# Moving the products of the first stage and the sums of the last two quads in a Strassen matmul with logsumexp

## The chip, the cores and the metric

The kernel runs on one core of a Trainium2 chip. The metric is the device time of one execution in microseconds (us). Three runs of the kernel before gave 423.86, 423.88 and 424.39 us.

## The reference

```python
m, k, n = 1024, 4096, 4096
def reference(a: np.ndarray, b: np.ndarray) -> np.ndarray:
    x = np.matmul(a, b)
    return special.logsumexp(x, axis=-1).astype(np.float32)
```

A is 1024 x 4096 and B is 4096 x 4096, both float32 with normal entries. The output is one number for each of the 1024 rows.

## The kernel before

**Tiles.** A has eight row tiles of 128 rows (m = 0 to 7), B has eight column blocks of 512 (nb = 0 to 7), and the inner dimension has 32 slices of 128 (k). Loads convert to float16. The sum over k stands in PSUM as float32; from each finished 128 x 512 piece VectorE takes the maximum (`lse_max`, L89, kept negative in `negmax`) and ScalarE the sum of exponentials (`lse_exp`, L94). At the end the pieces of a row are put together (`combine`).

**Head, block 0 (L255 to L326).** A must be transposed for TensorE. Its first six row tiles arrive in pieces of 128 rows x 4 slices. `arrivals` lists for each group of four slices (a round, eight rounds in all): A tile 0, B slices 0 and 1, A tile 1, B slices 2 and 3, A tiles 2 to 5. So there are 64 arrivals, eight a round. A piece of A is transposed by four TensorE instructions (`transpose_group`, L209) into one of two PSUM tiles in turn; even ones are copied out by VectorE (L220), odd ones by ScalarE (L222). `behind` then issues the products that an arrival makes possible (`plain`, L227: 128 x 128 by 128 x 512, one for each slice and row tile), and VectorE's sums of quarters of A (`a_sums_early`, `a_sums_late`), which the later blocks need. How far `behind` stays after the transposes is the lag: the list `back`. `warm` issues products of zeros while there is nothing else. The loads go out on POOL's queue, at most 12 pieces of A ahead, since they use 12 staging slots in `tb`.

**Strassen blocks (L334 to L578).** From block 1 on, two row tiles, a pair of slices and the two halves of a block of B are taken as 2 x 2 matrices. Seven products instead of eight suffice, each from sums of quarters. A quad q is two row tiles by one block: four quarters c11, c12 (one PSUM tile, `r0`) and c21, c22 (another, `r1`), each 128 x 256. Its products m1, m5, m2, m6, m3, m4, m7 have 16 instructions each (L395), about 1.745 us for one and 12.2 us for a quad. The quarters of A with their sums stay in `aT`, `s1`, `s2` and `s5`. The sums of B are made by VectorE, block by block, with `make`: t1 for m1, t6 for m6, t4 for m4 into `T1`, `T6`, `T4` (parts of `tb`), t3 for m3 and t7 for m7 in place in the loaded block. Each comes in four parts of 128 x 1024. t3 must follow t6, and t7 must follow t4 and t1, as they overwrite their inputs.

**Work around one quad.** ScalarE copies `r0` to `e` (L466) and c21 to `s` (L470), then `flush` issues the exponentials of the quad before (L94), then come the copies of c12 (L544) and c21 (L546) after m3 and m4. VectorE adds and subtracts in `s` (L480, L481), then `sub(x, x, s)`, the adds into c22 and c11 and the two maxima. `s` has one buffer for all quads. All of this is in an order written out by hand (`manual_schedule`); each engine takes its instructions in this order.

**Steps.** Step 0 is block 1 with quads 0 to 2, the first four products of the three quads interleaved as B arrives ("joint"). Steps 1 to 6 are blocks 2 to 7 with quads 0 to 3. Quad 3 consists of row tiles 6 and 7, which come later by a DMA transpose. Steps 7 and 8 are quad 3 of blocks 0 and 1, which are loaded again: block 0 (`again0`) with its sums in the space of `s1`, `s2` and `s5`, block 1 (`again1`, called `last`) with its data in the space of `aT` and its sums in `tb`. `early` is step 6, `joined` step 7, `tail` the last quad of a step whose following block's sums are made in it, `final` step 8.

**The order around the change.** In the last quad of step 0, VectorE makes the rest of block 2's sums; t7 and the maxima wait in `deferred` until the first add and subtract of the next quad. For the last two quads the sums are spread: in step 6 t1, t6 and t3 of block 0 follow quad 1, t4 comes in quad 2 and t7 behind it; three quarters of t1 and t6 of block 1 come in quad 3, with the last quarters; t3, t4 and t7 of block 1 come in step 7.

Of the kernel before, what the change touches and what calls it, by code (L numbers as in the profile page):

```python
# [13 lines left out]
def kernel(  # L14
# [19 lines left out]
    MT, KT, NB = M // P, K // P, N // FD  # L34
    MP, KP = MT // 2, KT // 2
    G = 4
    GI = KP // G
# [44 lines left out]
    def add(o, x, y):  # L82
        nc.vector.tensor_tensor(out=o, in0=x, in1=y, op=ALU.add)  # L83

    def sub(o, x, y):
        nc.vector.tensor_tensor(out=o, in0=x, in1=y, op=ALU.subtract)  # L86

    def lse_max(pt, m, nb):
        nc.vector.tensor_reduce(  # L89
            out=negmax[:, m, nb : nb + 1], in_=pt, axis=AX.X, op=ALU.max, negate=True  # L90
        )

    def lse_exp(pt, m, nb, scale=1.0):
        nc.scalar.activation(  # L94
            out=pt,
            in_=pt,
            func=AF.Exp,
            bias=negmax[:, m, nb : nb + 1],
            scale=scale,
            accum_out=tsum[:, m, nb : nb + 1],  # L100
        )
# [29 lines left out]
    class Block:  # L131
# [10 lines left out]
        def load(self, lo, hi):  # L142
            nc.gpsimd.dma_start(  # L143
                out=self.raw[lo // GI][:, lo % GI : lo % GI + hi - lo],
                in_=b_rows[:, lo:hi, :, ts(self.nb, FD)],
            )
# [56 lines left out]
    def transpose_group(k0, kn, m):  # L203
        src = stg.pop((k0, m))
        n = count[0]
        count[0] += 1
        pst = tps[n % 2]
        for j in range(kn):
            nc.tensor.matmul(  # L209
                pst[:, ts(j, P)],  # L210
                src[:, ts(j, P)],
                ident,
                is_transpose=True,
                start=(j == 0),
                stop=(j == kn - 1),
            )
        dst = aT[:, k0 // 2 : (k0 + kn) // 2, :, m // 2, m % 2, :]
        v = pst[:, 0 : kn * P].rearrange("p (i t c) -> p i t c", t=2, c=P)
        if n % 2 == 0:
            nc.vector.tensor_copy(out=dst, in_=v)  # L220
        else:
            nc.scalar.copy(out=dst, in_=v)  # L222
# [3 lines left out]
    def plain(pt, i, kp, m):  # L226
        nc.tensor.matmul(  # L227
            pt,
            aT[:, i, kp, m // 2, m % 2, :],
            blk0.raw[i // GI][:, i % GI, kp, :],  # L230
            start=(done[m] == 0),
            stop=(done[m] == KT - 1),
        )
        done[m] += 1

    def a_sums_early(r, q):
        a11, a12 = aT[:, r, 0, q, 0, :], aT[:, r, 1, q, 0, :]
        a21, a22 = aT[:, r, 0, q, 1, :], aT[:, r, 1, q, 1, :]
        add(s1[:, r, q], a11, a22)
        add(s2[:, r, q], a21, a22)  # L240
        add(s5[:, r, q], a11, a12)

    def a_sums_late(r, q):
        a11, a12 = aT[:, r, 0, q, 0, :], aT[:, r, 1, q, 0, :]
        a21, a22 = aT[:, r, 0, q, 1, :], aT[:, r, 1, q, 1, :]
        sub(a21, a21, a11)
        sub(a12, a12, a22)

    def first_max(m):
        lse_max(acc[m // 2][m % 2], m, 0)  # L250
        lse_exp(acc[m // 2][m % 2], m, 0)
# [13 lines left out]
    def behind(k0, kn, what, x):  # L265

        if what == "a":
            have_a.setdefault(k0, []).append(x)
            todo = [(k, x) for k in range(k0, k0 + kn) if k in have_b]
        else:  # L270
            have_b.update({k0: 1, k0 + 1: 1})
            todo = [(k, m) for k in (k0, k0 + 1) for m in have_a.get(x, [])]
        for k, m in todo:
            plain(acc[m // 2][m % 2], k // 2, k % 2, m)
        r = slice(k0 // 2, (k0 + kn) // 2)
        if what == "a":
            if x >= 3 and in_place:
                a_sums_late(*in_place.pop(0))
            if x % 2 == 1 and k0 + kn < KT:
                a_sums_early(r, x // 2)  # L280
            if x == 5:
                in_place.extend([(r, 0), (r, 1), (r, 2)])
            if k0 + kn == KT and x == 4:
                first_max(0)
                first_max(1)
                for what in ("t1", "t6"):
                    blk1.make(what, 0, 2)

    def warm(n):
        for _ in range(n):  # L290
            nc.tensor.matmul(acc[2][1], zeros[:, 0:P], zeros[:, 0:FD], start=True, stop=True)  # L291
# [17 lines left out]
    back = []  # L309
    for n, (k0, kn, what, x) in enumerate(arrivals):  # L310
        while coming and (coming[0][2] == "b" or loads[0] < count[0] + NSLOT):
            load(*coming.pop(0))
            if not coming:
                for lo in range(0, KP, 2):
                    blk1.load(lo, lo + 2)
        if what == "a":
            transpose_group(k0, kn, x)
        if k0 < KN and x < 3:
            warm(1)
        if len(back) == min(3, 1 + n // 8):  # L320
            behind(*back.pop(0))
        back.append((k0, kn, what, x))
    while back:
        behind(*back.pop(0))
    for m in range(2, MT - 2):
# [2 lines left out]


    pending = []  # L330
    deferred = []

    def flush():
        for f in pending:  # L334
# [9 lines left out]
    plan = [(lambda: blk1, range(MP - 1))]  # L344
# [3 lines left out]
    blk, nxt = None, blk1  # L348
    for step, (_, qs) in enumerate(plan):
        blk, nxt = nxt, None  # L350
        nb = blk.nb
        more = step + 1 < len(plan)
        early = more and plan[step + 1][0] is again0
        if more:
            if plan[step + 1][0] is again1:
                nxt = last
            else:
                nxt = plan[step + 1][0]()
# [24 lines left out]
        for q in qs:  # L383
# [5 lines left out]
            r0, r1 = quads[q]  # L389
# [11 lines left out]
                        skip_group_check=True,  # L401
                    )

            joined = step == len(plan) - 2
            tail = more and not early and not joined and q == qs[-1]
            final = not more
            if final:
                c22 = psum_pool.tile([P, FD], f32, name="c22", tag="ps")[:, 0:H]  # L410

# [59 lines left out]
            flush()  # L471
            if tail and not joint:
                nxt.make("t1")
            if early and q == MP - 1:
                for g in range(G - 1):
                    last.make("t1", g * GI, (g + 1) * GI)
            if joined:
                for what in ("t3", "t4"):
                    last.make(what)
            add(s[:, 2], s[:, 2], e[:, 1])  # L480
            sub(s[:, 0], s[:, 2], e[:, 0])  # L481
            for f in deferred:
                f()
            deferred.clear()
            if early and q == MP - 2:
                nxt.make("t4")
            if early and q == MP - 1:
                for g in range(G - 1):
                    last.make("t6", g * GI, (g + 1) * GI)
                for what in ("t1", "t6"):  # L490
                    last.make(what, KP - GI, KP)
            if joined:
                last.make("t7")
            if joint and q + 1 in quads:
                e_next = fix_pool.tile([P, 2, H], f32, name=f"e_{q}", tag="e")
                nc.scalar.copy(out=e_next, in_=halves(quads[q + 1][0]))
# [35 lines left out]
                sub(lg[:, m0:MT], lg[:, m0:MT], nmmin[:, m0:MT])  # L532
                continue
            if joint:
                for what in ("t1", "t6", "t3") if q == 0 else ("t1", "t6"):
                    nxt.make(what, q * GI, (q + 1) * GI)
            elif tail:
                nxt.make("t6")
                nxt.make("t3")
            if step == 1 and q == 2:  # L540
                a_sums_early(slice(KP // 2, KP), MP - 1)
                a_sums_late(slice(KP // 2, KP), MP - 1)
# [4 lines left out]
            m7(c11)  # L547
            sub(x, x, s[:, 0::2])
            add(c22, c22, x[:, 0])

            def maxima(r1=r1, r0=r0, q=q, nb=nb):
                for r, m in ((r1, 2 * q + 1), (r0, 2 * q)):
                    lse_max(r, m, nb)
                    pending.append(lambda r=r, m=m: lse_exp(r, m, nb))

            add(c11, c11, x[:, 1])
            if joint and tail:
                for what in ("t1", "t6"):
                    nxt.make(what, 3 * GI, KP)
                for g in range(1, G):  # L560
                    nxt.make("t3", g * GI, (g + 1) * GI)
                nxt.make("t4")
                deferred.extend([lambda b=nxt: b.make("t7"), maxima])
            else:
                if tail:
                    nxt.make("t4")
                    nxt.make("t7")
                maxima()
            if early and q == 1:
                for what in ("t1", "t6", "t3"):  # L570
                    nxt.make(what)
            if early and q == MP - 2:
                nxt.make("t7")
            if step == 1 and q == 1:
                a_sums_early(slice(0, KP // 2), MP - 1)
                a_sums_late(slice(0, KP // 2), MP - 1)
            if early and q == 1:
                last = again1().load_all()  # L578
# [32 lines left out]
```

## Time and profile before

| | |
|---|---|
| median of three runs | 423.88 us |
| the profiled execution | 424.39 us, span 422.6 us |
| TensorE products, weight loads | 412.7 us (98%), 348.4 us (82%) |
| VectorE, ScalarE, POOL | 258.7 us, 109.3 us, 74.3 us |
| first Strassen product starts | 62.83 us |
| step 1 starts | 99.57 us |
| step 7, step 8 start | 393.09 us, 405.31 us |
| last TensorE product ends | 417.7 us |

The span runs from the first to the last instruction. PE is TensorE, DVE is VectorE, ACT is ScalarE, PEld is TensorE's weight load. A line of the timeline has start and length in us, the engine, the line of the kernel, the operation, what it writes and reads, and in brackets how long the engine was idle ahead of it and what ended that. A line of the waits has the waiting engine, tile and line, what it waited for, the total in us, how often and the longest. A line of the chain of waits has start, length and the step.

### The profile page before, as it was taken

How to read it: one execution, taken by the hardware profiler on the slowest of the kernel's cores; microseconds unless marked ns; L12 is line 12 of the kernel's file. 1: busy time of each engine (PE TensorE's matmuls, PEld its weight loads, DVE VectorE, ACT ScalarE, POOL GpSimd, SP SyncE). 2: the span in 40 equal slices, each digit the busy share in tenths (PEclk: the TensorE clock that was granted, in tenths of full speed). 3: DMA queues.
4: the chain of work that ended last, by engine and by line, in shares of the span. 5: the costliest groups of instructions: out<-in, count | busy, mean ns of one | idle time of the engine just before them, and what ended most of it. 6: DMA issues, size and time to landing. Idle time of an engine off the chain costs nothing.

```text
span 422.6 us, 8529 instructions
## 1 busy us (share of the span) xinstructions
PE 412.7 (98%) x3647; PEld 348.4 (82%) x3647; DVE 258.7 (61%) x571; ACT 109.3 (26%) x278; POOL 74.3 (18%) x117
## 2 busy tenths in 40 slices
PE   6989999999999999999999999999999999999995
PEld 2545558888888888888888888888888888888884
DVE  1466777979646793257812694336832587299954
ACT  1222242132132221122222212222221222222223
POOL 7667763101001030003000030001100030110000
PEclk9999999999999999999999999999999999999999
DMA  8999999999999499102990079400990039799000
GB/s 117 197 201 199 202 205 207 207 207 215 190 195 187 69 169 207 24 2 41 207 152 2 2 115 208 79 2 2 192 205 3 2 62 207 132 199 198 3 2 0
DMA packets 57845, 52.97 MB, mean 125 GB/s; under 512 B 10192, under 2 KB 57296, under 8 KB 57808
## 3 DMA queue, kind: packets, MB, share of 16 engines
q0 software_dynamic: 49344, 50.34, 72.4%
q1 hardware_dynamic: 8464, 2.10, 3.5%
q8 instruction: 28, 0.46, 0.4%
q14 instruction: 9, 0.07, 0.1%
HBM read 100.66 MB, written 2.10 MB: 243 GB/s over the span
## 4 chain that ended last, share of the span: by engine, by line
PE 92%; DMA 4%; POOL 1%; DVE 1%; ACT 1%; issue 0%; DVEq 0%; ACTq 0%; POOLq 0%
DMA tb<-in_a_dram 3%; PE acc_1_0_1342 L395 2%; PE acc_1_0_764 L395 2%; PE acc_3_0_4470 L395 2%; PE acc_0_0_3386 L395 2%; PE acc_1_0_2974 L395 2%; PE acc_3_0_2150 L395 2%; PE acc_0_0_1766 L395 2%; PE acc_0_0_762 L395 2%; PE acc_1_0_4054 L395 2%; PE acc_2_0_3642 L395 2%; PE acc_3_0_4334 L395 2%; PE acc_0_0_3926 L395 2%; PE acc_3_0_2690 L395 2%; PE acc_2_0_2562 L395 2%; PE acc_0_0_1210 L395 2%
## 5 line engine op out<-in xcount | busy, mean ns | idle before, releaser
L395 PEld LDWEIGHTS <-aT 128*128 128x128 f16 x1856 | 181.5, 98 | 21.2
L395 PEld LDWEIGHTS <-s_71 128*128 128x128 f16 x464 | 45.4, 98 | 5.5
L395 PEld LDWEIGHTS <-s_73 128*128 128x128 f16 x464 | 45.4, 98 | 5.3
L395 PEld LDWEIGHTS <-s_72 128*128 128x128 f16 x464 | 45.4, 98 | 5.3
L209 PEld LDWEIGHTS <-tb 128*128 128x128 f16 x192 | 14.1, 98 | 16.5 <-DMA tb<-in_a_dram 8.2
L198 POOL DMA_DIRECT2D tb<-in_a_dram x48 | 26.0, 545 | 6.0 <-issue 2.1
L227 PEld LDWEIGHTS <-aT 128*128 128x128 f16 x192 | 16.8, 98 | 11.9 <-ACT aT L222 0.3
L220 DVE COPY aT<-tps_97 128x512 f16<-128x512 f16 x24 | 10.2, 425 | 25.4 <-PE tps_97 L209 25.2
L222 ACT COPY aT<-tps_98 128x512 f16<-128x512 f16 x24 | 14.0, 585 | 44.1 <-PE tps_98 L209 44.1
L86 DVE TENSOR_TENSOR aT<-aT 128x256 f16<-128x256 f16 (+1 forms) x56 | 16.2, 344 | 0.0
L209 PE MATMUL tps_97<-ident,tb 128*128 128x128 f16 x96 | 9.3, 220 | 2.8 <-DMA tb<-in_a_dram 2.8
L209 PE MATMUL tps_98<-ident,tb 128*128 128x128 f16 x96 | 9.3, 219 | 1.0 <-DMA tb<-in_a_dram 1.0
L83 DVE TENSOR_TENSOR s_71<-aT 128x256 f16<-128x256 f16 (+1 forms) x26 | 8.2, 317 | 3.0 <-ACT aT L222 2.0
L143 POOL DMA_DIRECT2D b_0_2838<-in_b_dram x1 | 0.9, 890 | 45.4 <-PE acc_3_0_2690 L395 45.4
L143 POOL DMA_DIRECT2D b_0_2298<-in_b_dram x1 | 0.9, 878 | 45.4 <-PE acc_3_0_2150 L395 45.4
L143 POOL DMA_DIRECT2D b_0_3378<-in_b_dram x1 | 0.9, 878 | 45.4 <-PE acc_3_0_3230 L395 45.4
L143 POOL DMA_DIRECT2D b_0_3918<-in_b_dram x1 | 0.9, 878 | 45.4 <-PE acc_3_0_3770 L395 45.4
L83 DVE TENSOR_TENSOR s_73<-aT 128x256 f16<-128x256 f16 (+1 forms) x26 | 8.3, 318 | 0.0
L83 DVE TENSOR_TENSOR s_72<-aT 128x256 f16<-128x256 f16 (+1 forms) x26 | 8.2, 317 | 0.0
L143 POOL DMA_DIRECT2D aT<-in_b_dram x4 | 3.5, 900 | 21.2 <-PE acc_1_0_4054 L395 21.2
L291 PE MATMUL acc_1_96<-s_73 128*128 128x512 f16 x15 | 5.8, 520 | 1.2 <-DVE s_73 L294 1.2
L83 DVE TENSOR_TENSOR tb<-aT 128x1024 f16<-128x1024 f16 x8 | 5.1, 687 | 1.0 <-DMA aT<-in_b_dram 1.0
(1047 smaller groups left out, 891.4 us busy)
## 6 DMA issues: line engine op xcount, KB each, us to landing
tb<-in_a_dram POOLq DMA_DIRECT2D x48, 128.0 KB, 5.9
aT<-in_b_dram POOLq DMA_DIRECT2D x4, 1024.0 KB, 15.2
b_0_83<-in_b_dram POOLq DMA_DIRECT2D x4, 256.0 KB, 5.9
b_1_84<-in_b_dram POOLq DMA_DIRECT2D x4, 256.0 KB, 6.7
b_2_85<-in_b_dram POOLq DMA_DIRECT2D x4, 256.0 KB, 6.2
b_3_86<-in_b_dram POOLq DMA_DIRECT2D x4, 256.0 KB, 6.2
b_0_87<-in_b_dram POOLq DMA_DIRECT2D x2, 512.0 KB, 8.6
b_1_88<-in_b_dram POOLq DMA_DIRECT2D x2, 512.0 KB, 11.8
```

Source lines behind the costliest of these rows:

```text
L83: nc.vector.tensor_tensor(out=o, in0=x, in1=y, op=ALU.add)
L86: nc.vector.tensor_tensor(out=o, in0=x, in1=y, op=ALU.subtract)
L143: nc.gpsimd.dma_start(out=self.raw[lo // GI][:, lo % GI : lo % GI + hi - lo], in_=b_rows[:, lo:hi, :, ts(self.nb, FD)],)
L198: nc.gpsimd.dma_start(out=slot, in_=a_m[m, :, k0 * P : (k0 + kn) * P])
L209: nc.tensor.matmul(pst[:, ts(j, P)], src[:, ts(j, P)], ident, is_transpose=True, start=(j == 0), stop=(j == kn - 1),)
L220: nc.vector.tensor_copy(out=dst, in_=v)
L222: nc.scalar.copy(out=dst, in_=v)
L227: nc.tensor.matmul(pt, aT[:, i, kp, m // 2, m % 2, :], blk0.raw[i // GI][:, i % GI, kp, :], start=(done[m] == 0), stop=(done[m] == KT - 1),)
L291: nc.tensor.matmul(acc[2][1], zeros[:, 0:P], zeros[:, 0:FD], start=True, stop=True)
L395: nc.tensor.matmul(c, lhs(i), rhs(i), start=(start and i == 0), stop=(i == KP - 1), skip_group_check=True,)
```

## The change

There are three edits.

- In the head the lag is `min(3, 1 + n // 24)` instead of `min(3, 1 + n // 8)`: one for the first 24 arrivals, two for the next 24, then three. In the first two rounds (n < 16) the list is also emptied each time that a piece of B arrives.
- In step 0, t3 of block 2's first quarter is no longer made in quad 0. In its last quad all of t3, then t4, t7 and both maxima are issued at once; `deferred` is gone. In all quads but such last ones, the maximum of `r1` is taken before the last add into c11 instead of after it.
- For the last two quads the sums are no longer spread: block 0's t1 and t6 are made in quad 2 of step 6, t3 and t4 in quad 3, t7 at its end. Block 1's are all made in step 7, as in any other last quad of a step.

```diff
-        if len(back) == min(3, 1 + n // 8):
+        if len(back) == min(3, 1 + n // 24):
             behind(*back.pop(0))
         back.append((k0, kn, what, x))
+        while back and n < 2 * MT and what == "b":
+            behind(*back.pop(0))
...
-            joined = step == len(plan) - 2
-            tail = more and not early and not joined and q == qs[-1]
-            final = not more
+            tail, final = more and not early and q == qs[-1], not more
...
             if tail and not joint:
                 nxt.make("t1")
-            if early and q == MP - 1:
-                for g in range(G - 1):
-                    last.make("t1", g * GI, (g + 1) * GI)
-            if joined:
-                for what in ("t3", "t4"):
-                    last.make(what)
+            if early and q == MP - 2:
+                nxt.make("t1")
+                nxt.make("t6")
             add(s[:, 2], s[:, 2], e[:, 1])
             sub(s[:, 0], s[:, 2], e[:, 0])
-            for f in deferred:
-                f()
-            deferred.clear()
-            if early and q == MP - 2:
-                nxt.make("t4")
-            if early and q == MP - 1:
-                for g in range(G - 1):
-                    last.make("t6", g * GI, (g + 1) * GI)
-                for what in ("t1", "t6"):
-                    last.make(what, KP - GI, KP)
-            if joined:
-                last.make("t7")
...
             if joint:
-                for what in ("t1", "t6", "t3") if q == 0 else ("t1", "t6"):
+                for what in ("t1", "t6"):
                     nxt.make(what, q * GI, (q + 1) * GI)
             elif tail:
                 nxt.make("t6")
                 nxt.make("t3")
+            if early and q == MP - 1:
+                nxt.make("t3")
+                nxt.make("t4")
...
-
-            def maxima(r1=r1, r0=r0, q=q, nb=nb):
-                for r, m in ((r1, 2 * q + 1), (r0, 2 * q)):
-                    lse_max(r, m, nb)
-                    pending.append(lambda r=r, m=m: lse_exp(r, m, nb))
-
+            if not tail:
+                lse_max(r1, 2 * q + 1, nb)
             add(c11, c11, x[:, 1])
             if joint and tail:
                 for what in ("t1", "t6"):
                     nxt.make(what, 3 * GI, KP)
-                for g in range(1, G):
-                    nxt.make("t3", g * GI, (g + 1) * GI)
+                nxt.make("t3")
+            if tail:
                 nxt.make("t4")
-                deferred.extend([lambda b=nxt: b.make("t7"), maxima])
-            else:
-                if tail:
-                    nxt.make("t4")
-                    nxt.make("t7")
-                maxima()
-            if early and q == 1:
-                for what in ("t1", "t6", "t3"):
-                    nxt.make(what)
-            if early and q == MP - 2:
+            if tail or (early and q == MP - 1):
                 nxt.make("t7")
+            if tail:
+                lse_max(r1, 2 * q + 1, nb)
+            lse_max(r0, 2 * q, nb)
+            for r, m in ((r1, 2 * q + 1), (r0, 2 * q)):
+                pending.append(lambda r=r, m=m, nb=nb: lse_exp(r, m, nb))
```

More of the change, by code (lines that the diff above doesn't have):

```diff
@@ L330 @@
     pending = []
-    deferred = []
     def flush():
```

## The prediction

> **What bounds the kernel now.** I read the page's busy times first, then TensorE's waits, then the chain of waits, then the timelines of the three places that the change touches: the head (0 to 63 us), the seam after the first Strassen block (100 to 124 us) and the end (388 to 420 us).
>
> ```profile
> span 422.6 us, 8529 instructions
> ...
> PE 412.7 (98%) x3647; PEld 348.4 (82%) x3647; DVE 258.7 (61%) x571; ACT 109.3 (26%) x278; POOL 74.3 (18%) x117
> ```
>
> ```profile
> PE tps_97 L209 <- DMA tb<-in_a_dram: 2.8, 3, 1.5
> PE acc_1_96 L291 <- DVE s_73 L294: 1.2, 1, 1.2
> PE tps_98 L209 <- DMA tb<-in_a_dram: 1.0, 1, 1.0
> ```
>
> TensorE is idle for 9.9 us of the span: 5 us in these waits, all before 24.2 us, and 4.9 us after its last product (417.7 to 422.6). In between it never stops for more than 0.1 us. The number and shapes of the products don't change, so the change can only move those 9.9 us or open new holes.
>
> Head, in the chain of waits: a load, its landing, and the transposes that start 0.05 us later.
>
> ```profile
> 17.21 6.89 DMA tb<-in_a_dram
> 24.10 0.05 issue
> 24.15 0.40 PE tps_97 L209 x4
> ```
>
> Seam, in the timelines of VectorE, ScalarE and TensorE. The sums for block 2 end at 104.92 + 0.69; t7 and the two maxima of the last quad come only behind the first add of the next quad. In the quad after that, the four exponentials delay one copy (L544), and TensorE starts m7 at 122.36, 0.06 us after this copy ends and 0.08 us after m4 was done (120.53 + 1.745).
>
> ```profile
> 104.92 0.69 DVE L86 TENSOR_TENSOR tb<-b_3_747 128x1024 f16<-128x1024 f16 x1
> 107.16 0.43 DVE L83 TENSOR_TENSOR s_0_1212<-s_0_1212 128x256 f32<-128x256 f32 x1 [1.55 <-ACT s_0_1212 L470]
> 107.97 0.68 DVE L83 TENSOR_TENSOR b_0_744<-b_0_744 128x1024 f16<-128x1024 f16 x1
> ...
> 110.37 0.68 DVE L89 TENSOR_REDUCE negmax<-acc_2_1_767 128x1 f32<-128x512 f32 x1
> ```
>
> ```profile
> 108.50 0.37 ACT L544 COPY s_0_1212<-acc_0_0_1210 128x256 f32<-128x256 f32 x1 [1.37 <-PE acc_0_0_1210 L395]
> ...
> 121.91 0.39 ACT L544 COPY s_1_1344<-acc_1_0_1342 128x256 f32<-128x256 f32 x1
> ```
>
> End, in VectorE's timeline. It idles 4.07 us in the last quad; from the maximum at 414.65 the path is a string of short VectorE and ScalarE operations to 419.64, none of which waits for TensorE.
>
> ```profile
> 388.91 0.42 DVE L86 TENSOR_TENSOR s_3_4336<-s_3_4336 128x256 f32<-128x256 f32 x1
> ...
> 411.20 0.43 DVE L83 TENSOR_TENSOR s_3_4613<-s_3_4613,e_last 128x256 f32<-128x256 f32 x1 [4.07 <-ACT s_3_4613 L470]
> ...
> 414.65 0.42 DVE L89 TENSOR_REDUCE negmax<-acc_3_0_4610 128x1 f32<-128x256 f32 x1 [0.55 <-ACT s_3_4613 L505]
> ...
> 419.64 0.16 DVE L86 TENSOR_TENSOR lg<-lg,nmmin 128x2 f32<-128x2 f32 x1 [0.54 <-ACT lg L531]
> ```
>
> **What the Trainium skill says.** Perfetto Trace Analysis, "Identifying the Most-Contended Engine": matmul busy time overstates how near TensorE is to its peak, and the share of weight loads is the better sign. Here the two are 98% and 82%; I use TensorE's holes, not its share. VectorE: DVE Perf Modes, "Mode 2×_1P — pack two bf16 into one 32-bit read": a two-tensor add of 16-bit data makes two results a cycle. At the page's 0.96 GHz that is an estimate of 533 ns for a 1024-column sum; the trace has 601 ns from start to start (eight sums from 370.37 to 375.18), and I use 601. PSUM — Partial Sum Buffer, "Terms": two engines on one bank at once is an error. The trace agrees that m7 is held for the copy of the other half of its bank: 122.30 to 122.36.
>
> **Part 1, the head: -0.1 us (ends -0.3 and +0.9).** Lag means how many arrivals the products stay behind the transposes. Nothing is added; the order of products and transposes changes. The loads are issued by POOL in the same order, and POOL waits there for landings of earlier loads (such as 0.53 us before the issue at 16.34), while the loads run at 200 to 204 GB/s with no pause; so the landings stay, and faster products cannot hurry them. From arrival 48 on both orders are the same (lag 3), and the third tile of A in round 7 lands at 44.03 + 5.9 = 49.93 us; its transposes start at 50.24. So 0.3 us is the most that the head can give. What it can lose: with a lag of one, only one group of transposes (0.22 us) or one product group (0.86 us) covers the copy out of PSUM. From the start of the transposes to the end of the copy are 0.43 + 0.58 = about 1.05 us on ScalarE and 0.85 on VectorE. Walked in the new order from the same landings: products of the second tile follow its transposes directly in round 2 (a wait of 0.84), the third tile's have 0.22 + 0.22 us of cover (0.4), the second tile's of round 3 wait 0.4 again. Against that, at the transposes of 24.15 eight products that could run were still queued in the old order and four are in the new one: 4 x 0.215 = 0.86 us are done before. I get the third tile of round 3 at 24.4 with four products to come, some 0.6 us ahead; of this, rounds 4 to 6 (lag 2) lose about 0.5 in landings and copies. Net -0.1.
>
> **Part 2, the seam: +0.9 us (ends 0 and +1.2).** t3 of the first quarter moves from the first quad to here, and t7 and the maxima are no longer put behind the next quad's first add. VectorE, from the end of the last add (99.77 + 0.34 = 100.11): t1 and t6 of the last quarter 2 x 0.60, t3, t4 and t7 four each, 12 x 0.601 = 7.21, so 108.53; first maximum ready at 108.53 + 0.68 = 109.21, the second, 0.60 behind, at 109.81. Queued on ScalarE behind L470 are now the two exponentials that need these: 109.24 and 109.92 (0.68 apart), then at 110.58 the copy L544, which ran at 108.50. It ends at 110.95, m7 starts at 111.02 instead of 110.05: +0.97 us on TensorE, which has no slack behind it. The 0.08 us hole at 122.36 closes, since only two exponentials stand there: +0.89. All sums are still early enough for their products: t3 at 103.7 for m3 at 106.56, t4 at 106.1 for 108.31, t7 at 108.5 for 110.05. The low end is that the copy is not what m7 waits for; the high end adds what a few late semaphores could.
>
> **Part 3, the sums for the last two quads: +3.0 us (ends +2.2 and +3.6).** Before, everything for block 0's last quad and three quarters of the last t1 are done when VectorE reaches 389.25. After, only t1 and t6 of block 0 are: t3, t4, t7 (12 x 0.601 = 7.21) and three of t1 (1.9) come later, 9.1 us more work in the last two quads. Step by step from 389.25, without a wait: t3, t4 4.81; three quad operations and a maximum (0.72, 0.34, 0.60, 0.34), t7 2.41, a maximum 0.60: 399.07. Then t1 of the last block 2.41, add and subtract 0.80, t6, t3 4.82, quad operations 1.40, t4, t7 4.82, two maxima 1.20: 414.52. In the profile before this point is 411.20; so it comes 3.3 us later. The further path takes 3.45 us to the maximum, of which some 0.35 are a wait for m3 that is covered now: it stands at 417.6 instead of 414.65, +3.0. Everything behind it is VectorE and ScalarE in turn and moves with it. TensorE is not held: t1 is ready at 401.5 for 405.31, t6 at 404.7 for 410.55, t3 at 407.1 for 412.30, t4 at 410.9 for 414.05, t7 at 413.3 for 415.79. Low end: VectorE overlaps more than these intervals show; high end: one more late semaphore per group.
>
> The maxima of ordinary quads move before the last add (0.60 us later for c11): free, since the copy that needs it (360.14) comes over 3 us after it (356.61). No DMA moves; the loads of the last block wait on POOL for TensorE at 368.6, 20 us before use.
>
> **Sum.** -0.1 + 0.9 + 3.0 = +3.8 us: span 426.4. The profiled execution took 424.39 us (1.8 around its span), 0.51 above the median of 423.88; carried to the median, 427.7.
>
> **The rivals.** *The head gives it back.* If the loads follow TensorE's pace (each reuses a buffer that a transpose frees), the earlier products pull the stream and the 3.8 us of DMA waits go: 423.88 + 3.8 - 3.7 = 424.0, no change. For it: POOL shows some waits on TensorE (up to 0.41 us). Against: they are small, and bandwidth is flat. It decides from landings 3 us earlier by round 3. *One seam is hidden*: the copy does not hold m7, or the last quad absorbs a third of part 3: 423.88 + 2.9 = 426.8. *The head loses too*: each copy at lag one holds TensorE and nothing comes back: +0.9 instead of -0.1, 428.7. *It does not do what it says*: the scheduler could have put the sums back early; the order of instructions built from the new code shows VectorE's queue as I walked it, so this is nearly out.
>
> **How the numbers follow.** The three parts as read 0.66 (427.2 to 428.2), one hidden 0.14, head loses 0.12, head gives it back 0.06, anything else 0.02. The range 426.2 to 428.9 holds the first three. 0.2% is 0.85 us, about what can be told from no change: slower 0.92, within it 0.05, faster 0.03.
>
> **What would show it.** Right: a hole of about 1 us on TensorE before m7 in the first quad after the seam, with two exponentials just ahead of the copy; no idle on VectorE from 389 us to the last quad's first add; TensorE's last product to the end growing from 4.9 to about 7.9 us; the first Strassen product within 0.3 us of 62.83. Wrong: that product 2 us earlier, or idle time left on VectorE in the last quad.

## The result and the profile after

The changed kernel took 428.90 us (median, 428.63 to 429.22) against 424.09 us (423.86 to 424.39) for the kernel before in the same comparison: a ratio of 1.0113, 95% interval 1.0096 to 1.0131, so 4.8 us slower (4.1 to 5.6). The profiled execution took 429.22 us with a span of 427.4 us, 4.8 us more than before's.

The head of the page, then its shares of the chain that ended last. Before, that chain was 92% TensorE and 1% VectorE.

```profile
span 427.4 us, 8527 instructions
...
PE 414.6 (97%) x3647; PEld 349.0 (82%) x3647; DVE 260.5 (61%) x571; ACT 109.0 (26%) x278; POOL 74.5 (17%) x117
```

```profile
PE 84%; DVE 10%; ACT 2%; DMA 1%; issue 1%; POOL 1%; DVEq 0%; ACTq 0%; POOLq 0%
```

TensorE's waits (waiting tile and line, what it waited for, total us, times, longest):

```profile
PE acc_1_96 L291 <- DVE s_73 L294: 1.2, 1, 1.2
PE acc_1_92 L227 <- ACT aT L222: 1.2, 3, 0.7
PE acc_0_91 L227 <- DMA b_0_83<-in_b_dram: 1.1, 1, 1.1
PE acc_0_0_1216 L396 <- ACT s_0_1218 L529: 0.8, 1, 0.8
PE acc_0_93 L227 <- DVE aT L220: 0.3, 1, 0.3
```

The waits for loads of A (3.8 us) are gone from the head. In their place stand waits for the copies out of PSUM and one for an early load of B. The fourth line is new, after the seam: it is the hole ahead of m7. (Line numbers behind the head's loop, from about L320 on, differ between kernels: L396 here is L395 before, L529 is L544.)

Because TensorE runs without a pause between fixed points, I compare the stages by the starts of their first products:

| stage | before, us | after, us | change |
|---|---|---|---|
| head, to the first Strassen product | 62.83 | 63.48 | +0.65 |
| step 0 | 36.74 | 36.94 | +0.20 |
| step 1, first quad | 12.23 | 13.19 | +0.96 |
| step 1, second quad | 12.30 | 12.23 | -0.07 |
| from there to the start of the last product (m7 of step 8) | 291.69 | 291.69 | 0 |
| its start to the end of the last VectorE operation | 4.01 | 7.10 | +3.09 |

The sum is +4.83 us, as the times say. (In the runs' comparisons below the last row is taken from start to start, which is 0.16 us shorter: 3.85 before, 6.94 after.)

The seam after, VectorE and ScalarE:

```profile
108.78 0.69 DVE L83 TENSOR_TENSOR b_3_747<-b_3_747 128x1024 f16<-128x1024 f16 x1
109.38 0.69 DVE L89 TENSOR_REDUCE negmax<-acc_2_1_767 128x1 f32<-128x512 f32 x1
109.98 0.69 DVE L89 TENSOR_REDUCE negmax<-acc_2_0_766 128x1 f32<-128x512 f32 x1
110.58 0.42 DVE L83 TENSOR_TENSOR s_0_1218<-s_0_1218 128x256 f32<-128x256 f32 x1
```

```profile
110.11 0.66 ACT L94 ACTIVATE acc_2_1_767<-acc_2_1_767,negmax 128x512 f32<-128x512 f32 x1 [2.13 <-DVE negmax L89]
...
110.79 0.65 ACT L94 ACTIVATE acc_2_0_766<-acc_2_0_766,negmax 128x512 f32<-128x512 f32 x1
...
111.45 0.37 ACT L529 COPY s_0_1218<-acc_0_0_1216 128x256 f32<-128x256 f32 x1
```

```profile
111.87 0.60 PE L396 MATMUL acc_0_0_1216<-b_0_744,aT 128*128 128x256 f16 x4 [0.80 <-ACT s_0_1218 L529]
```

The copy ends at 111.82, m7 starts at 111.87 where 110.90 would have been free (m4 is done then). At the end, VectorE's queue has no pause from 390.19 to the short operations at 418.51:

```profile
390.19 0.43 DVE L83 TENSOR_TENSOR s_3_4324<-s_3_4324 128x256 f32<-128x256 f32 x1 [5.71 <-ACT s_3_4324 L467]
...
412.90 2.49 DVE L83 TENSOR_TENSOR aT<-aT 128x1024 f16<-128x1024 f16 x4
...
416.50 0.42 DVE L83 TENSOR_TENSOR s_3_4613<-s_3_4613,e_last 128x256 f32<-128x256 f32 x1
...
419.49 0.42 DVE L89 TENSOR_REDUCE negmax<-acc_3_0_4610 128x1 f32<-128x256 f32 x1
...
424.47 0.16 DVE L86 TENSOR_TENSOR lg<-lg,nmmin 128x2 f32<-128x2 f32 x1 [0.55 <-ACT lg L513]
```

The 4.07 us of idle time at the first add of the last quad (416.50) are gone, and the maximum at 419.49 no longer waits for the copy.

### The profile page after: what moved, and what is told of

It reads as the page before. It is cut to its first block, busy times and chain, and to the rows that moved or that the text cites. A ratio compares the mean times of both kernels' runs of the same rounds, so it can differ in the third digit from the quotient of the medians.

```text
span 427.4 us, 8527 instructions
## 1 busy us (share of the span) xinstructions
PE 414.6 (97%) x3647; PEld 349.0 (82%) x3647; DVE 260.5 (61%) x571; ACT 109.0 (26%) x278; POOL 74.5 (17%) x117
## 4 chain that ended last, share of the span: by engine, by line
PE 84%; DVE 10%; ACT 2%; DMA 1%; issue 1%; POOL 1%; DVEq 0%; ACTq 0%; POOLq 0%
PE acc_1_92 L227 2%; PE acc_0_93 L227 2%; PE acc_2_0_766 L396 2%; PE acc_3_0_2690 L396 2%; PE acc_3_0_3770 L396 2%; PE acc_2_0_3102 L396 2%; PE acc_0_0_2306 L396 2%; PE acc_1_0_1894 L396 2%; PE acc_2_0_1477 L396 2%; PE acc_2_0_4186 L396 2%; PE acc_1_0_3514 L396 2%; PE acc_0_0_3386 L396 2%; PE acc_1_0_2974 L396 2%; PE acc_3_0_2150 L396 2%; PE acc_1_0_4054 L396 2%; PE acc_0_0_3926 L396 2%
## 5 line engine op out<-in xcount | busy, mean ns | idle before, releaser
L396 PEld LDWEIGHTS <-aT 128*128 128x128 f16 x1856 | 181.5, 98 | 22.3 <-issue 1.3
L396 PEld LDWEIGHTS <-s_71 128*128 128x128 f16 x464 | 45.4, 98 | 5.5
L396 PEld LDWEIGHTS <-s_73 128*128 128x128 f16 x464 | 45.4, 98 | 5.3
L396 PEld LDWEIGHTS <-s_72 128*128 128x128 f16 x464 | 45.4, 98 | 5.3
```

The lines of the kernel that those rows point to most:

```text
L396: nc.tensor.matmul(c, lhs(i), rhs(i), start=(start and i == 0), stop=(i == KP - 1), skip_group_check=True,)
```

## The experiments

Every kernel is the kernel before with the edit shown; e7_seam_exp and e9_seam_max also have the edit of e3_seam, e8_tail_t3 has that of e2_tail, and e11_tail_t3_t6 that of e8_tail_t3. The times are medians beside the kernel before on the same chip. The ratio is an estimate of its own, with its 95% interval, and can differ a little from the ratio of the two medians; differences in us below come from it.

| run | time, us | before, us | ratio |
|---|---|---|---|
| e1_head | 424.63 | 424.31 | 1.0008 (1.0000 to 1.0016) |
| e2_tail | 427.34 | 424.31 | 1.0074 (1.0055 to 1.0093) |
| e3_seam | 425.10 | 424.31 | 1.0013 (1.0007 to 1.0020) |
| e4_maxorder | 424.49 | 424.31 | 1.0002 (0.9994 to 1.0010) |
| e5_flush | 424.42 | 424.20 | 1.0001 (0.9990 to 1.0012) |
| e6_lag | 423.94 | 424.20 | 0.9994 (0.9981 to 1.0007) |
| e7_seam_exp | 424.68 | 424.20 | 1.0007 (0.9994 to 1.0021) |
| e8_tail_t3 | 426.27 | 424.20 | 1.0043 (1.0030 to 1.0057) |
| e9_seam_max | 424.23 | 424.15 | 0.9999 (0.9991 to 1.0007) |
| e10_tailback | 425.43 | 424.15 | 1.0030 (1.0018 to 1.0043) |
| e11_tail_t3_t6 | 425.17 | 424.15 | 1.0027 (1.0015 to 1.0039) |
| e12_end | 423.86 | 424.15 | 0.9997 (0.9989 to 1.0005) |

Single executions of one kernel spread over 1 us and more, and the stage lengths show where: in nine profiles with the old head, the first Strassen product starts between 61.95 us (e3_seam) and 64.25 us (e2_tail). Behind it, the same code takes the same time to 0.02 us in every profile. So the head is judged by times alone, everything else by stage lengths.

### The head

```diff
-        if len(back) == min(3, 1 + n // 8):
+        if len(back) == min(3, 1 + n // 24):
             behind(*back.pop(0))
         back.append((k0, kn, what, x))
+        while back and n < 2 * MT and what == "b":
+            behind(*back.pop(0))
```

> Only the head is changed: the new lag and the emptying of the list when B arrives. The two profiles have the first Strassen product at 62.83 us (before) and 63.48 us (after), +0.65. Theory 1, the products have come to depend on the copies out of PSUM and on the early landings of B, and nothing later gives that back: +0.4 to +0.7 us in the time, and the copies show as waits of TensorE of about 0.2 to 0.7 us in rounds 1 to 6. Theory 2, as predicted, the order costs nothing and the 0.65 us came from loads that landed 0.5 us later in that one execution: -0.2 to +0.2 us.

Measured: +0.34 us (0 to 0.68), with the first Strassen product at 63.08. Its waits are those of the changed kernel, in TensorE's timeline (the line's own idle time in brackets):

```profile
16.83 1.47 PE L227 MATMUL acc<-b,aT 128*128 128x512 f16 x6 [0.68 <-ACT aT L222]
19.04 1.04 PE L227 MATMUL acc<-b,aT 128*128 128x512 f16 x4 [0.30 <-DVE aT L220]
24.24 0.60 PE L227 MATMUL acc<-b,aT 128*128 128x512 f16 x2 [0.25 <-ACT aT L222]
```

The three waits stand with the same lengths in the changed kernel and in e10_tailback, whose heads ended at 63.48 and 62.52. The interval reaches both theories; three new heads have a mean of 63.03, nine old ones 62.69, a difference that is less than the spread.

The traces show where the loss lies. In the profiles before and after, the first transposes of round 2 start at the same time with the same products done. Then come the transposes of the third tile of round 3; first before:

```profile
14.65 0.39 PE L209 MATMUL tps_97<-ident,tb 128*128 128x128 f16 x4
...
24.15 0.40 PE L209 MATMUL tps_97<-ident,tb 128*128 128x128 f16 x4 [1.17 <-DMA tb<-in_a_dram]
```

and after:

```profile
14.65 0.39 PE L209 MATMUL tps_97<-ident,tb 128*128 128x128 f16 x4
...
25.08 0.39 PE L209 MATMUL tps_97<-ident,tb 128*128 128x128 f16 x4
```

After, four more products are done by then, worth 0.86 us, so the new order is 0.07 us behind there. It loses another 0.57 us in rounds 4 to 6, where TensorE waits 0.19 us for a copy once a round. In all three profiles with the new head, the stretch from the first transposes of round 2 to the first Strassen product took 48.83 to 48.93 us, with no wait for a load longer than 0.1 us. With the old head the loads set the pace, and it took 47.72 to 49.53 us (mean 48.25). Where round 2 starts depends on the early landings: between 13.59 and 14.65 us with the new head, between 13.79 and 14.87 us with the old one.

The two halves of the edit alone, first the `while` and then the new divisor:

> Half of the head: the list is emptied when a piece of B arrives in the first 16 arrivals, the lag stays min(3, 1 + n // 8). If the exposure to the early landings of B and to the copies in round 2 (0.68 and 0.30 us in the profile after) is the cost, most of the head's cost is here: +0.3 to +0.6 us. If the long lag of one in rounds 2 to 6 is the cost, nothing is here: -0.1 to +0.1 us.

> The other half of the head: lag min(3, 1 + n // 24), no emptying. If the copies under a lag of one and two are the cost (0.24, 0.19, 0.19 and 0.19 us in rounds 3 to 6 in the profile after), +0.2 to +0.5 us are here. If they are covered by work done earlier, as predicted, -0.2 to +0.1 us.

Measured +0.05 us (-0.4 to +0.5) and -0.25 us (-0.8 to +0.3). Neither half is told from nothing, so which of them costs is left open. The emptying alone carries the 0.68 us wait for ScalarE's copy in round 2, and then one of 1.15 us for A at 24.13, much as in the kernel before (1.17 at 24.15): there the loads set the pace again, and from there to the first Strassen product it took 38.68 us, as before: the waits in round 2 were covered.

### The order of the maxima

```diff
-            def maxima(r1=r1, r0=r0, q=q, nb=nb):
+            def maxima(r1=r1, r0=r0, q=q, nb=nb, tail=tail):
                 for r, m in ((r1, 2 * q + 1), (r0, 2 * q)):
-                    lse_max(r, m, nb)
+                    if r is r0 or tail:
+                        lse_max(r, m, nb)
...
+            if not tail:
+                lse_max(r1, 2 * q + 1, nb)
             add(c11, c11, x[:, 1])
```

> Only the order of the maximum of r1 and the last add into c11 is swapped, in quads that are not the last of a step. Theory 1, in the joint quads of step 0 the next quad's copy into the one buffer s waits for this add, so each of the two seams between them comes 0.3 to 0.6 us later on ScalarE and TensorE waits 0.2 us ahead of m7 of the second quad: +0.2 us, nothing in the other steps. Rival, as predicted: nothing, -0.1 to +0.1 us.

The time says +0.1 us (-0.25 to +0.4), which decides nothing. Step 0 decides: it took 36.95 us, as in the changed kernel (36.94), against 36.74 in all the kernels with the old order. Only a joint quad pays: the first four products of the joint quads are finished early, so the copy into `s` follows the last add of the quad before at once. ScalarE's line in the kernel before and in the changed kernel:

```profile
89.75 0.37 ACT L470 COPY s_1_1066<-acc_1_1_765 128x256 f32<-128x256 f32 x1 [1.90 <-DVE acc_0_0_762 L83]
```

```profile
90.92 0.37 ACT L467 COPY s_1_1065<-acc_1_1_765 128x256 f32<-128x256 f32 x1 [2.41 <-DVE acc_0_0_762 L83]
```

Less the 0.65 us by which this execution's head was later, the copy comes 0.52 us later; m7 of the second quad waits 0.26 (e4_maxorder) instead of 0.06 us. The third quad's m7 is not held in either.

### The seam

```diff
-                for what in ("t1", "t6", "t3") if q == 0 else ("t1", "t6"):
+                for what in ("t1", "t6"):
...
-                for g in range(1, G):
-                    nxt.make("t3", g * GI, (g + 1) * GI)
+                nxt.make("t3")
                 nxt.make("t4")
-                deferred.extend([lambda b=nxt: b.make("t7"), maxima])
+                nxt.make("t7")
+                maxima()
```

> Only the last quad of step 0 is changed: t3 whole, t7 and the maxima at once instead of behind the next quad's first add. Theory 1, two exponentials wait for the late maxima and hold the copy of c12, and this copy holds m7: a hole of 0.97 us ahead of m7 in step 1's first quad, the 0.07 us hole in its second quad gone, +0.9 us. Rival, the hole is paid by something that would wait anyway: +0.2 us or less.

Measured: +0.55 us (0.3 to 0.85); the first quad of step 1 takes 13.18 us, +0.95 us as in the changed kernel. The next quad gives 0.07 us back, so the stages say +0.88, just above the interval; the medians differ by 0.79. For the mechanism, the exponentials were then put behind the copies:

```diff
-            flush()
+            if not (step == 1 and q == 0):
+                flush()
...
             nc.scalar.copy(out=x[:, 1], in_=c21)
+            if step == 1 and q == 0:
+                flush()
```

> The seam of the third run again, but in step 1's first quad the two exponentials are issued behind the two copies of c12 and c21 instead of ahead of them. Theory 1, the copy behind the exponentials holds m7: the hole of 0.97 us is gone, and the time is that of the kernel before, -0.1 to +0.1 us. Rival, m7 waits for VectorE's late sums (t7, or the add into s) itself: the hole stays, +0.5 to +0.9 us.

Theory 1 failed here. The quad takes 12.84 us, so 0.61 of the 0.95 us stay. ScalarE waits with nothing ahead of the copy, and VectorE shows for what:

```profile
109.66 0.37 ACT L545 COPY s<-acc 128x256 f32<-128x256 f32 x1 [3.11 <-PE acc L395]
```

```profile
109.15 0.42 DVE L83 TENSOR_TENSOR s<-s 128x256 f32<-128x256 f32 x1
```

ScalarE's wait is put down to TensorE, but m3 was done 1.9 us earlier. The copy writes `x[:, 0]`, which is the second quarter of `s`; VectorE's `add(s[:, 2], s[:, 2], e[:, 1])` still reads this quarter as `e[:, 1]`, and ends at 109.57. So the same copy has two holders: the exponentials (which wait for the maxima) and this add (which is queued behind the maxima). If that is so, deferring the maxima alone must remove the whole hole, with t3 and t7 still made at once as in e3_seam:

```diff
-                deferred.extend([lambda b=nxt: b.make("t7"), maxima])
+                nxt.make("t7")
+                deferred.append(maxima)
```

> The seam once more: t3 and t7 of block 2 at once as in the third run, but the two maxima of step 0's last quad stay behind the next quad's add and subtract. In the seventh run, with the exponentials moved away, m7 was still held 0.45 us longer than in the kernel before: the copy of c12 writes the half of s that VectorE's add still reads, and this add stood behind t7 and both maxima (109.15 us). Theory 1a, both the exponentials and this add hold the copy: here the add comes at about 108 us, no exponential stands ahead of the copy, and step 1's first quad takes 12.2 to 12.3 us instead of 13.18 (third run) and 12.84 (seventh run). Theory 1b, t7 made at once holds m7 by itself: 12.8 us or more.

Measured: 12.23 us, no hole, and the time of the kernel before. The add is early again, and the copy follows it:

```profile
107.98 0.42 DVE L83 TENSOR_TENSOR s<-s 128x256 f32<-128x256 f32 x1
```

```profile
108.48 0.37 ACT L544 COPY s<-acc 128x256 f32<-128x256 f32 x1 [1.92 <-DVE s L83]
```

### The sums for the last two quads

The edit is that of the change to `joined`, `early` and `last`, except that t7 of block 0 follows both maxima instead of the first.

```diff
-            joined = step == len(plan) - 2
-            tail = more and not early and not joined and q == qs[-1]
+            tail = more and not early and q == qs[-1]
...
+            if early and q == MP - 2:
+                nxt.make("t1")
+                nxt.make("t6")
...
+            if early and q == MP - 1:
+                nxt.make("t3")
+                nxt.make("t4")
...
+            if early and q == MP - 1:
+                nxt.make("t7")
```

> Only the sums for the last two quads are put back to steps 6 and 7. Theory 1, VectorE's queue sets the end: 9.1 us of sums more behind step 6's last quad, against 5.9 us of idle time and 0.35 us of slack, +3.0 to +3.2 us, all of it after the last product on TensorE. Theory 2, a part of the +4.8 us that is not accounted for by the other places (about 1 us) sits here too: +4 us. Rival, the idle time absorbs it: under +1 us.

Measured: +3.1 us (2.3 to 3.9), and 6.78 us from the last product's start to the last operation's, +2.93. Theory 1 holds; the 1 us by which the forecast was short is not here. Then single items were taken out of the crowded queue. First t3 of block 0, moved to quad 2 of step 6:

```diff
                 nxt.make("t6")
+                nxt.make("t3")
             add(s[:, 2], s[:, 2], e[:, 1])
...
             if early and q == MP - 1:
-                nxt.make("t3")
                 nxt.make("t4")
```

> The tail of the second run with one item moved: t3 of block 0 (four sums, 4 x 0.601 = 2.4 us of VectorE) in quad 2 of step 6, where VectorE is idle, instead of quad 3. Theory 1, in the last two quads VectorE never pauses, so each us of sums taken out comes off the end: 2.4 us less than the second run, +0.7 us against the kernel before. Rival, the end is set by the chain from t1, t6, t3 of block 1 to the products: as the second run, or no more than 0.5 us less.

Measured: +1.8 us (1.3 to 2.4) and 5.95 us at the end: only 0.83 us less for 2.4 us of sums. Both expectations missed. VectorE got 0.96 us of new idle time ahead of step 7's first add, and 0.20 us ahead of the subtraction in step 6's last quad:

```profile
391.74 0.69 DVE L86 TENSOR_TENSOR s<-s 128x512 f32<-128x512 f32 x1 [0.20 <-ACT s L536]
...
400.48 0.42 DVE L83 TENSOR_TENSOR s<-s 128x256 f32<-128x256 f32 x1 [0.96 <-ACT s L469]
```

The other 0.4 us of the 1.57 that are missing are gaps of 0.1 to 0.2 us between operations. So what counts may be the work behind the last idle time. To see this, t6 of block 1 was moved ahead of this add as well:

```diff
+            if step == len(plan) - 2:
+                nxt.make("t6")
             add(s[:, 2], s[:, 2], e[:, 1])
...
-                nxt.make("t6")
+                if step != len(plan) - 2:
+                    nxt.make("t6")
                 nxt.make("t3")
```

> The eighth run (t3 of block 0 moved to quad 2 of step 6) with one more item moved: t6 of block 1 ahead of step 7's first add, into the 0.96 us that VectorE idles there. In the eighth run the end came only 0.84 us earlier, against 2.4 us of sums taken out, since new idle time of 0.96 us appeared ahead of that add. Theory 1, the work left behind the last idle time sets the end: from the last product's start to the end 5.95 us in the eighth run, 5.0 us here, +1.1 us against the kernel before. Rival, a later wait takes its place: 5.5 us or more.

Measured: the 0.96 us are gone, 4.90 us at the end, and +1.1 us (0.6 to 1.7) in the time. The order is worth 1.05 us with not one operation more or less.

### The sum of the places, and the end by itself

The changed kernel with the sums for the last two quads as before (the edits of e1_head, e3_seam and e4_maxorder together):

> The changed kernel with the sums of the last two quads spread as in the kernel before. If the four places add up: the order of the maxima 0.21, the seam 0.96 - 0.07, the head 0 to 0.65, so +1.1 to +1.7 us against the kernel before, and from the last product's start to the end 3.85 us as before. If the places act on each other (the head's lateness hides a seam), under +0.9 us. The first Strassen product gives one more sample of the new head: within 61.9 to 64.3 us, the spread of the old head over six profiles, if the head's cost is below that spread.

Measured: +1.3 us (0.8 to 1.8); step 0 36.94, first quad 13.19, end 3.85 us. The places add up.

Last, an edit of its own in the kernel before, since its end is a string of short waits:

```diff
-                combine(m0, m0 + 1, NB)
+                combine(m0, m0 + 1, NB,
+                        between=lambda: lse_max(c21, m0 + 1, NB),
+                        behind_ln=lambda: add(y, y, c21))
...
-                lse_max(c21, m0 + 1, NB)
-                add(y, y, c21)
```

(`behind_ln` is called behind the logarithm in `combine`.)

> The kernel before with the end's string of short operations put closer: the maximum of c21 runs while ScalarE makes the exponential of the first combine, and the add into y while it makes the logarithm (waits of 0.28 and 0.27 us on VectorE in the kernel before). Expected 0.4 us less after the last product (3.85 to 3.4 us), limited by that product's end at 417.70: -0.4 us in the time, at the edge of what can be told. Rival: the two operations (0.34 us each) are longer than the gaps and push the chain: 0 to +0.1 us.

In the profile the end shrinks from 3.85 to 3.40 us, as expected: VectorE's two waits in the first combine are filled.

```profile
416.27 0.42 DVE L89 TENSOR_REDUCE negmax<-acc 128x1 f32<-128x256 f32 x1
416.62 0.17 DVE L124 TENSOR_TENSOR d<-d,tsum 128x8 f32<-128x8 f32 x1
```

In the time it is -0.1 us (-0.5 to +0.2): the head's spread hides it. It is not shown to be faster than the kernel before.

## Why the prediction was right, and what it got wrong

The direction was right, and so were the mechanism at the end and most of that at the seam. The size was too small by 1.0 us: +3.8 forecast, +4.8 measured. 428.9 us is the top of the range, and two of the four runs lie above it (429.09 and 429.22), so that it still falls inside is luck.

- **Part 3, the end: right.** +3.0 forecast, +3.09 measured, and TensorE was not held. The walk was 0.24 us early at the last quad's first add: an operation that needs the one just ahead of it on VectorE came 0.46 to 0.47 us after it (416.50, 416.96, 417.42), where the walk took 0.34 in some places. e8_tail_t3 also shows the limit of counting work against idle time: the idle time has to lie where the work is taken out.
- **Part 2, the seam: the size right, the cause half right.** +0.97 forecast for the hole and -0.08 for the next one, +0.96 and -0.07 measured. But the step "Queued on ScalarE behind L470 are now the two exponentials" named one holder of two. The add in `s`, which the walk left out, holds the copy for 0.61 us by itself (e7_seam_exp), and the exponentials add 0.34. Both go when only the maxima are deferred (e9_seam_max). The size came out all the same because the holder that was named is the later one: in the changed kernel the add ends at 111.00, and the exponentials let the copy start at 111.45.
- **The maxima of ordinary quads: wrong.** "Free" was argued from a step in which the next copy comes 3 us later. In step 0's joint quads it comes at once: +0.21 us (step 0 in e4_maxorder, +0.20 in the changed kernel).
- **Part 1, the head: the waits right, the lead wrong.** -0.1 forecast, +0.65 in the profile, and 0 to +0.68 by the time of e1_head, so the forecast lies just outside. The walk's waits for copies (0.84, 0.4, 0.4, and about 0.5 in rounds 4 to 6) are there: counted as the walk does, from the start of the transposes to the first product that uses them less the work that covers this time, they are 0.84, 0.46 and 0.41 us, then 0.57. (The brackets of the timeline show 0.68, 0.30 and 0.25, as they count from the end that the profile gives to the work in between.) What failed is the lead of "some 0.6 us" at the third tile of round 3, put at 24.4 us: it came at 25.08, 0.07 us behind the old order. With the walk's own waits, 32 products of 0.215 us and eight groups of transposes of 0.22 us, 24.4 needs a round 2 that starts at 14.1. It started at 14.65, since the second piece of B landed at 3.92 + 5.87 us instead of 3.92 + 5.42, and in the new order its products stand ahead of the next transposes. In e1_head, where this piece took 5.47 us, round 2 started at 14.24 and the third tile of round 3 at 24.68, still 0.28 us later than the walk says. So about 0.4 us of the error came with the landing in this one execution, and 0.3 us are the walk's own.

The signs that were named show the same. The hole, the two exponentials ahead of the copy, VectorE without a pause to the last quad's first add, and 8.0 us from the last product's end to the end of the span came as forecast. The first Strassen product within 0.3 us of 62.83 did not (63.48), but the old head alone spreads over 2.3 us, so one profile could not have told this.

In the two profiles, the missing 1.0 us are 0.75 from the head, 0.2 from the maxima and 0.1 from the end. How much of the head's 0.75 is usual is known only to the width of e1_head's interval. Of the rivals, the head that gives it back is out: loads did not come 3 us earlier (POOL issued B's pieces for round 3 at 14.78 and 16.70 us, before at 14.38 and 16.34). The hidden seam is out too, and VectorE's queue stands in the trace as it was walked, so the scheduler did not put the sums back. The head that loses is the one that comes nearest: copies at lag one do hold TensorE, 2.28 us behind the start of round 2, where before it waited 1.65 us for loads (counted in the same way). Its loss is smaller than the 0.9 us that this rival had.

## What to carry to other kernels

A wait can be held twice, as the copy at the seam was. Take away one holder in the order and look again before you call it the cause. Moving work off a crowded queue pays only as far as no idle time opens behind the place it is taken from (0.83 us for 2.4 us of sums in e8_tail_t3): look for the last idle time first, and put work there. An order that costs nothing in the steady part can cost at a seam, where the next writer of a single buffer comes at once. And a walk from the landings of one execution should be done again with a landing half a us later.

## What the runs showed of the hardware that was not expected

The same head, with the same code, ended anywhere between 61.95 and 64.25 us in nine executions, while the stages behind it, some 356 us, repeated to 0.02 us each wherever their code was the same. The first ten products of zeros took 4.08 us in one execution (before) and 4.45 us in another (e12_end), and the first four transposes behind them 0.39 and 0.63 us. These products came 0.41 to 0.42 us apart, against 0.22 us for later products of the same shape, while the profile shows a granted clock of 1.00 for this stretch too. The wait of an engine was put down in one view to the engine that released something last by name, not to the one that held it (ScalarE's copy in e7_seam_exp, 3.11 us "for TensorE" of which 1.9 us were VectorE's); the release shows in the timeline of the other engine.
